# Layer normalisation on one core: tiles of 12 rows in place of 8, and a second first load on another queue

## The chip, the core and the metric

The kernel runs on one core of a Trainium2 chip. The metric is the device time of one execution, in microseconds (us). Before the change the median of three runs is 317.96 us (317.96 to 318.17).

## The reference

The input x has 32 x 512 rows of 1024 float32 values. Each row is normalised by its own mean and variance; there is no scale and no offset.

```python
mean = np.mean(x, axis=-1, keepdims=True)
var = np.var(x, axis=-1, keepdims=True)
return ((x - mean) / np.sqrt(var + eps)).astype(np.float32)      # eps = 1e-5
```

So 16384 rows of 4 KB, 67.11 MB, are read once and written once.

## The kernel before

**Tiles.** "Rows" of a tile are counted per partition. A tile of K rows is 128 x K rows of x, laid so that each of the 128 partitions holds K rows that lie one after the other in memory (`rows_of`, L58): for each partition one run of 4K KB, on both sides of a transfer. `TILES` (L10) lists the 20 tiles: 2, 2, 4, then fourteen of 8, then 4, 2, 2; together 128 rows per partition.

**Ring.** All tiles live in one buffer `ring` of 48 rows per partition (L55). `place` (L17) gives each tile its position, from the front again when the end is reached. A tile is normalised in place and stored from where it lies, so a load may start only when the stores of the tiles that lay in its rows have landed.

**Order.** The kernel is written under a manual schedule: each engine carries out its own instructions in the order of the program, and waits on semaphores for the others. For each tile the loop at L121 to L126 issues the load from SP's queue (L122), works on the tile in one group of up to 8 rows (`group`, L71), and issues the store from ScalarE's queue (L126). SP has nothing but loads, so it runs ahead as far as the ring lets it. In what follows L0, L1, ... are the loads and S0, S1, ... the stores of the tiles, counted from 0.

**A group of G rows.**
1. VectorE takes the statistics of each half row, 2G instructions (L75, `stats`).
2. GpSimd (POOL) joins the four partial means and sums of squares of each row in nine small instructions in a row (L64 to L100, `half`, `nmean`, `dev`, `ss`).
3. ScalarE takes the square root (L103, `std`), VectorE the reciprocal (L107, `rstd`), POOL the product of the mean and the reciprocal (L109, `nmr`).
4. ScalarE scales and shifts each row in place, G instructions (L111).

VectorE's reciprocal stands in its order ahead of the next tile's statistics, so VectorE waits in step 2 of each tile. The small tiles come from a pool with four buffers of each (`st`, L49).

Of the kernel before, what the change touches and what calls it, by code (L numbers as in the profile page):

```python
# [1 line left out]

# [4 lines left out]


TILES = (2, 2, 4) + (8,) * 14 + (4, 2, 2)  # L10

RING = 48

GROUP = 8


def place(tiles, ring):  # L17

    plan, row, pos = [], 0, 0
    for K in tiles:  # L20
        if pos + K > ring:
            pos = 0
        plan.append((K, row, pos))
        row += K
        pos += K
    return plan


@with_exitstack
def kernel(  # L30
    ctx: ExitStack,
    tc: tile.TileContext,
    x: bass.AP,
    eps: bass.AP,
    out: bass.AP,
):
    nc = tc.nc
    P = nc.NUM_PARTITIONS
    eps_val = float(eps) if not isinstance(eps, bass.AP) else 1e-5

    x2 = x.flatten_outer_dims()
    o2 = out.flatten_outer_dims()
    N, D = x2.shape
    BN_MAX = nc.vector.BN_STATS_FMAX
    NSUB = D // BN_MAX
    assert sum(TILES) * P == N

    rings = ctx.enter_context(tc.tile_pool(name="rings", bufs=1))
    st = ctx.enter_context(tc.tile_pool(name="st", bufs=4))  # L49

    fdt = mybir.dt.float32
    AF = mybir.ActivationFunctionType
    ALU = mybir.AluOpType

    ring = rings.tile([P, RING, D], fdt)  # L55
    eps_t = rings.tile([P, 1], fdt)

    def rows_of(a, row, K):  # L58
        return a[row * P : (row + K) * P].rearrange("(p k) d -> p k d", p=P)

    def pool_sum(o, terms):
        G = terms.shape[1]
        half = st.tile([P, GROUP, 2], fdt, name="half")
        nc.gpsimd.tensor_tensor(  # L64
            out=half[:, :G], in0=terms[:, :, 0:2], in1=terms[:, :, 2:4], op=ALU.add
        )
        nc.gpsimd.tensor_tensor(  # L67
            out=o, in0=half[:, :G, 0], in1=half[:, :G, 1], op=ALU.add
        )

    def group(xs, G):  # L71
        stats = st.tile([P, GROUP, NSUB, 6], fdt, name="stats")
        for k in range(G):
            for s in range(NSUB):
                nc.vector.bn_stats(  # L75
                    out=stats[:, k, s, :],
                    in_=xs[:, k, s * BN_MAX : (s + 1) * BN_MAX],
                )

        H = 2 * NSUB  # L80
        parts = stats[:, :G].rearrange("p g s (h c) -> p g (s h) c", h=2)
        mean4, m2 = parts[:, :, :, 1], parts[:, :, :, 2]
        nmean = st.tile([P, GROUP], fdt, name="nmean")
        dev = st.tile([P, GROUP, H], fdt, name="dev")
        ss = st.tile([P, GROUP], fdt, name="ss")
        pool_sum(nmean[:, :G], mean4)
        nc.gpsimd.tensor_scalar(  # L87
            out=nmean[:, :G], in0=nmean[:, :G], scalar1=-1.0 / H, scalar2=None, op0=ALU.mult
        )
        nc.gpsimd.tensor_tensor(  # L90
            out=dev[:, :G],
            in0=mean4,
            in1=nmean[:, :G].unsqueeze(2).to_broadcast([P, G, H]),
            op=ALU.add,
        )
        nc.gpsimd.tensor_mul(out=dev[:, :G], in0=dev[:, :G], in1=dev[:, :G])  # L96
        nc.gpsimd.tensor_scalar(  # L97
            out=dev[:, :G], in0=dev[:, :G], scalar1=float(D // H), scalar2=None, op0=ALU.mult
        )
        nc.gpsimd.tensor_tensor(out=dev[:, :G], in0=dev[:, :G], in1=m2, op=ALU.add)  # L100
        pool_sum(ss[:, :G], dev[:, :G])
        std = st.tile([P, GROUP], fdt, name="std")
        nc.scalar.activation(  # L103
            out=std[:, :G], in_=ss[:, :G], func=AF.Sqrt, bias=eps_t, scale=1.0 / D
        )
        rstd = st.tile([P, GROUP], fdt, name="rstd")
        nc.vector.reciprocal(out=rstd[:, :G], in_=std[:, :G])  # L107
        nmr = st.tile([P, GROUP], fdt, name="nmr")
        nc.gpsimd.tensor_mul(out=nmr[:, :G], in0=nmean[:, :G], in1=rstd[:, :G])  # L109
        for k in range(G):  # L110
            nc.scalar.activation(  # L111
                out=xs[:, k, :],
                in_=xs[:, k, :],
                func=AF.Identity,
                bias=nmr[:, k : k + 1],
                scale=rstd[:, k : k + 1],
            )

    with tc.manual_schedule():
        nc.vector.memset(eps_t, eps_val)  # L120
        for K, row, pos in place(TILES, RING):  # L121
            nc.sync.dma_start(out=ring[:, pos : pos + K, :], in_=rows_of(x2, row, K))  # L122
            for g in range(0, K, GROUP):
                G = min(GROUP, K - g)
                group(ring[:, pos + g : pos + g + G, :], G)
            nc.scalar.dma_start(out=rows_of(o2, row, K), in_=ring[:, pos : pos + K, :])  # L126


# [1 line left out]
_INS = ['x', 'eps']  # L130
_OUTS = [((32, 512, 1024), 'float32')]

_NUMBERS = {'eps': 1e-05}


# [26 lines left out]
```

## Time and profile before

| What | us | Where it is from |
|---|---|---|
| median of three runs | 317.96 | the times |
| the profiled execution | 317.86 | the times |
| its span, first to last instruction or packet | 316.1 | the page |
| VectorE busy | 157.1 | the page, engines |
| ScalarE busy | 154.3 | the page, engines |
| POOL busy | 45.1 | the page, engines |
| statistics of 8 rows, 16 instructions | 9.59 | the timeline of VectorE |
| scaling of 8 rows, 8 instructions | 9.16 | the timeline of ScalarE |
| an 8-row load, issue to landing, median | 47.3 | the page, DMA issues |
| an 8-row store, issue to landing, median | 40.7 | the page, DMA issues |

The span is shorter than the execution's own time by 1.76 us, which lies outside of what the profile follows. Queue q1 holds the loads that SP issues, q10 the stores that ScalarE issues; 16 DMA engines move the packets of both. Beside the page, the trace holds a record of each DMA packet with its queue, size, start and duration. A transfer of K rows per partition appears there as 128 packets of 4K KB, 8 on each engine, and a packet of 4 bytes on each engine that tells of completion.

### The profile page before, as it was taken

The page shows a single profiled execution, that of the slowest core. Times are in us where ns is not written, and L with a number is a line of the kernel's source. Part 1 is how long each engine was busy: PE and PEld are TensorE (multiplying, and loading weights), DVE is VectorE, ACT ScalarE, POOL GpSimd, SP SyncE. Part 2 cuts the span into 40 slices and gives each one's busy share as a digit, 9 for nine tenths or more (in the row PEclk, how much of TensorE's full clock was granted, in tenths as well). Part 3 has the DMA queues.
Part 4 walks back from the last instruction along what each step waited for, and adds up shares of the span by engine and source line. Part 5 has one row for each costly group of instructions (what it writes and reads, how often), then busy time and mean ns, then how long its engine had stood idle before and what let it go on. Part 6 is the DMA issues. An engine that isn't in the chain of part 4 may idle for free.

```text
span 316.1 us, 794 instructions
## 1 busy us (share of the span) xinstructions
DVE 157.1 (50%) x277; ACT 154.3 (49%) x149; POOL 45.1 (14%) x204
## 2 busy tenths in 40 slices
DVE  2368596547092561916529074190652908363030
ACT  1336296692833809247091561900651956196321
POOL 0420202201102020020200202002020020221120
DMA  7999999999999999999999999999999999999996
GB/s 301 433 399 469 431 416 425 433 427 444 420 448 419 444 419 444 435 427 444 419 448 415 448 424 440 423 448 419 444 423 440 423 435 429 446 428 417 455 411 282
DMA packets 5766, 134.27 MB, mean 425 GB/s; under 512 B 640, under 2 KB 640, under 8 KB 640
## 3 DMA queue, kind: packets, MB, share of 16 engines
q1 hardware_dynamic: 2880, 67.11, 49.6%
q10 hardware_dynamic: 2880, 67.11, 49.3%
q14 instruction: 6, 0.05, 0.0%
HBM read 67.11 MB, written 67.11 MB: 425 GB/s over the span
## 4 chain that ended last, share of the span: by engine, by line
DMA 58%; DVE 17%; ACT 9%; POOL 6%; issue 3%; another core or an unknown queue 3%; ACTq 0%; POOLq 0%; DVEq 0%; SPq 0%
DMA ring<-in_x_dram 32%; DMA out_dram<-ring 27%; DVE stats L75 17%; ACT ring L111 8%; POOL half L64 1%; ACT std L103 1%; POOL dev L97 1%; POOL nmean L87 1%; POOL dev L100 1%; POOL dev L90 1%; POOL dev L96 1%; POOL nmean L67 1%; POOL ss L67 1%; DVE rstd L107 0%
## 5 line engine op out<-in xcount | busy, mean ns | idle before, releaser
L75 DVE BATCH_NORM_STATS2 stats<-ring 128x6 f32<-128x512 f32 x256 | 153.7, 678 | 71.2 <-DMA ring<-in_x_dram 71.2
L111 ACT ACTIVATE ring<-ring,nmr,rstd 128x1024 f32<-128x1024 f32 x128 | 147.0, 1227 | 10.8 <-POOL nmr L109 10.8
L103 ACT ACTIVATE std<-ss,eps_t 128x8 f32<-128x8 f32 (+2 forms) x20 | 6.0, 300 | 143.0 <-POOL ss L67 115.8
L107 DVE RECIPROCAL rstd<-std 128x8 f32<-128x8 f32 (+2 forms) x20 | 3.9, 193 | 77.3 <-ACT std L103 77.3
L64 POOL TENSOR_TENSOR half<-stats 128x16 f32<-128x16 f32 (+2 forms) x20 | 4.5, 226 | 221.0 <-DVE stats L75 221.0
L109 POOL TENSOR_TENSOR nmr<-nmean,rstd 128x8 f32<-128x8 f32 (+2 forms) x20 | 4.0, 202 | 27.2 <-DVE rstd L107 27.2
L97 POOL TENSOR_SCALAR dev<-dev 128x32 f32<-128x32 f32 (+2 forms) x20 | 5.6, 281 | 1.8
L100 POOL TENSOR_TENSOR dev<-dev,stats 128x32 f32<-128x32 f32 (+2 forms) x20 | 4.9, 243 | 1.7
L90 POOL TENSOR_TENSOR dev<-stats,nmean 128x32 f32<-128x32 f32 (+2 forms) x20 | 4.6, 231 | 1.7
L87 POOL TENSOR_SCALAR nmean<-nmean 128x8 f32<-128x8 f32 (+2 forms) x20 | 4.6, 228 | 1.8
L96 POOL TENSOR_TENSOR dev<-dev 128x32 f32<-128x32 f32 (+2 forms) x20 | 4.6, 228 | 1.6
L64 POOL TENSOR_TENSOR half<-dev 128x16 f32<-128x16 f32 (+2 forms) x20 | 4.2, 210 | 1.6
L67 POOL TENSOR_TENSOR nmean<-half 128x8 f32<-128x8 f32 (+2 forms) x20 | 4.0, 199 | 1.6
L67 POOL TENSOR_TENSOR ss<-half 128x8 f32<-128x8 f32 (+2 forms) x20 | 4.0, 199 | 1.6
L103 ACT ACT_TABLE_LOAD x1 | 1.3, 1283 | 0.9 <-DVE eps_t L120 0.9
L120 DVE MEMSET eps_t<- 128x1 f32 x1 | 0.1, 59 | 0.8 <-PEq L143 0.8
L143 POOL MEMSET const-float32-0.0<- 128x1 f32 x1 | 0.1, 98 | 0.2 <-issue 0.2
L143 POOL MEMSET const-uint8-127<- 128x1 uint8 x1 | 0.1, 102 | 0.0
L143 POOL MEMSET const-bfloat16-1.0<- 128x1 bf16 x1 | 0.1, 101 | 0.0
L143 POOL MEMSET const-float32-1.0<- 128x1 f32 x1 | 0.1, 98 | 0.0
## 6 DMA issues: line engine op xcount, KB each, us to landing
ring<-in_x_dram SPq DMA_DIRECT2D x14, 4096.0 KB, 47.3
out_dram<-ring ACTq DMA_DIRECT2D x14, 4096.0 KB, 40.7
ring<-in_x_dram SPq DMA_DIRECT2D x4, 1024.0 KB, 30.8
ring<-in_x_dram SPq DMA_DIRECT2D x2, 2048.0 KB, 27.2
out_dram<-ring ACTq DMA_DIRECT2D x4, 1024.0 KB, 16.7
out_dram<-ring ACTq DMA_DIRECT2D x2, 2048.0 KB, 24.5
```

The source lines that it names most:

```text
L64: nc.gpsimd.tensor_tensor(out=half[:, :G], in0=terms[:, :, 0:2], in1=terms[:, :, 2:4], op=ALU.add)
L67: nc.gpsimd.tensor_tensor(out=o, in0=half[:, :G, 0], in1=half[:, :G, 1], op=ALU.add)
L75: nc.vector.bn_stats(out=stats[:, k, s, :], in_=xs[:, k, s * BN_MAX : (s + 1) * BN_MAX],)
L87: nc.gpsimd.tensor_scalar(out=nmean[:, :G], in0=nmean[:, :G], scalar1=-1.0 / H, scalar2=None, op0=ALU.mult)
L90: nc.gpsimd.tensor_tensor(out=dev[:, :G], in0=mean4, in1=nmean[:, :G].unsqueeze(2).to_broadcast([P, G, H]), op=ALU.add,)
L96: nc.gpsimd.tensor_mul(out=dev[:, :G], in0=dev[:, :G], in1=dev[:, :G])
L97: nc.gpsimd.tensor_scalar(out=dev[:, :G], in0=dev[:, :G], scalar1=float(D // H), scalar2=None, op0=ALU.mult)
L100: nc.gpsimd.tensor_tensor(out=dev[:, :G], in0=dev[:, :G], in1=m2, op=ALU.add)
L103: nc.scalar.activation(out=std[:, :G], in_=ss[:, :G], func=AF.Sqrt, bias=eps_t, scale=1.0 / D)
L107: nc.vector.reciprocal(out=rstd[:, :G], in_=std[:, :G])
L109: nc.gpsimd.tensor_mul(out=nmr[:, :G], in0=nmean[:, :G], in1=rstd[:, :G])
L111: nc.scalar.activation(out=xs[:, k, :], in_=xs[:, k, :], func=AF.Identity, bias=nmr[:, k : k + 1], scale=rstd[:, k : k + 1],)
```

## The change

- The tiles are 4, 8, then nine of 12, then 6 and 2: 13 tiles in place of 20. The ring keeps 48 rows, four tiles of 12.
- A group takes up to 12 rows (`GROUP`). In the last four tiles (`LAST`) a group takes up to 6 (`FINE`), so the last two tiles of 12 are worked on in two groups each, with one store for both. There are 15 groups in place of 20.
- The first two loads are issued ahead of the loop, that of the second tile (8 rows) from ScalarE's queue, beside the first (4 rows) from SP's queue. The other loads stay on SP's queue.
- All small tiles but `stats` move to a pool with 15 buffers of each (`sm`).
- `place` is written out in the function, and `H` is computed outside of `group`; both give the same as before.

```diff
-TILES = (2, 2, 4) + (8,) * 14 + (4, 2, 2)
+TILES = (4, 8, 12, 12, 12, 12, 12, 12, 12, 12, 12, 6, 2)
 
 RING = 48
 
-GROUP = 8
+GROUP = 12
+FINE = 6
+LAST = 4
...
     st = ctx.enter_context(tc.tile_pool(name="st", bufs=4))
+    sm = ctx.enter_context(tc.tile_pool(name="sm", bufs=len(TILES) + 2))
...
-        half = st.tile([P, GROUP, 2], fdt, name="half")
+        half = sm.tile([P, GROUP, 2], fdt, name="half")
...
-        nmean = st.tile([P, GROUP], fdt, name="nmean")
-        dev = st.tile([P, GROUP, H], fdt, name="dev")
-        ss = st.tile([P, GROUP], fdt, name="ss")
+        nmean = sm.tile([P, GROUP], fdt, name="nmean")
+        dev = sm.tile([P, GROUP, H], fdt, name="dev")
+        ss = sm.tile([P, GROUP], fdt, name="ss")
...
+    def load(queue, K, row, pos):
+        queue.dma_start(out=ring[:, pos : pos + K, :], in_=rows_of(x2, row, K))
...
     with tc.manual_schedule():
         nc.vector.memset(eps_t, eps_val)
-        for K, row, pos in place(TILES, RING):
-            nc.sync.dma_start(out=ring[:, pos : pos + K, :], in_=rows_of(x2, row, K))
-            for g in range(0, K, GROUP):
-                G = min(GROUP, K - g)
+        for t, (K, row, pos) in enumerate(plan[:2]):
+            load(nc.scalar if t == 1 else nc.sync, K, row, pos)
+        for t, (K, row, pos) in enumerate(plan):
+            if t > 1:
+                load(nc.sync, K, row, pos)
+            step = FINE if t >= len(TILES) - LAST else GROUP
+            for g in range(0, K, step):
+                G = min(step, K - g)
                 group(ring[:, pos + g : pos + g + G, :], G)
             nc.scalar.dma_start(out=rows_of(o2, row, K), in_=ring[:, pos : pos + K, :])
```

`std`, `rstd` and `nmr` move to `sm` in the same way.

More of the change, by code (lines that the diff above doesn't have):

```diff
@@ L7 @@
 from concourse._compat import with_exitstack
-TILES = (2, 2, 4) + (8,) * 14 + (4, 2, 2)
+TILES = (4, 8, 12, 12, 12, 12, 12, 12, 12, 12, 12, 6, 2)
 RING = 48
-GROUP = 8
[L17 to L26, printed above, removed]
+GROUP = 12
+FINE = 6
+LAST = 4
 @with_exitstack
@@ L45 @@
     NSUB = D // BN_MAX
+    H = 2 * NSUB
     assert sum(TILES) * P == N
@@ L78, in group @@
                 )
-        H = 2 * NSUB
         parts = stats[:, :G].rearrange("p g s (h c) -> p g (s h) c", h=2)
         mean4, m2 = parts[:, :, :, 1], parts[:, :, :, 2]
-        nmean = st.tile([P, GROUP], fdt, name="nmean")
-        dev = st.tile([P, GROUP, H], fdt, name="dev")
-        ss = st.tile([P, GROUP], fdt, name="ss")
+        nmean = sm.tile([P, GROUP], fdt, name="nmean")
+        dev = sm.tile([P, GROUP, H], fdt, name="dev")
+        ss = sm.tile([P, GROUP], fdt, name="ss")
         pool_sum(nmean[:, :G], mean4)
@@ L101, in group @@
         pool_sum(ss[:, :G], dev[:, :G])
-        std = st.tile([P, GROUP], fdt, name="std")
+        std = sm.tile([P, GROUP], fdt, name="std")
         nc.scalar.activation(
@@ L105, in group @@
         )
-        rstd = st.tile([P, GROUP], fdt, name="rstd")
+        rstd = sm.tile([P, GROUP], fdt, name="rstd")
         nc.vector.reciprocal(out=rstd[:, :G], in_=std[:, :G])
-        nmr = st.tile([P, GROUP], fdt, name="nmr")
+        nmr = sm.tile([P, GROUP], fdt, name="nmr")
         nc.gpsimd.tensor_mul(out=nmr[:, :G], in0=nmean[:, :G], in1=rstd[:, :G])
@@ L117, in group @@
             )
+    def load(queue, K, row, pos):
+        queue.dma_start(out=ring[:, pos : pos + K, :], in_=rows_of(x2, row, K))
+    plan, row, pos = [], 0, 0
+    for K in TILES:
+        if pos + K > RING:
+            pos = 0
+        plan.append((K, row, pos))
+        row += K
+        pos += K
     with tc.manual_schedule():
         nc.vector.memset(eps_t, eps_val)
-        for K, row, pos in place(TILES, RING):
-            nc.sync.dma_start(out=ring[:, pos : pos + K, :], in_=rows_of(x2, row, K))
-            for g in range(0, K, GROUP):
-                G = min(GROUP, K - g)
+        for t, (K, row, pos) in enumerate(plan[:2]):
[6 more added lines that the diff above has]
+                G = min(step, K - g)
                 group(ring[:, pos + g : pos + g + G, :], G)
```

## The prediction

> **What bounds the kernel now.** I read the page first, its spans, engine shares and the two DMA rows:
>
> ```profile
> span 316.1 us, 794 instructions
> ...
> DVE 157.1 (50%) x277; ACT 154.3 (49%) x149; POOL 45.1 (14%) x204
> ...
> DMA  7999999999999999999999999999999999999996
> GB/s 301 433 399 469 431 416 425 433 427 444 420 448 419 444 419 444 435 427 444 419 448 415 448 424 440 423 448 419 444 423 440 423 435 429 446 428 417 455 411 282
> ...
> q1 hardware_dynamic: 2880, 67.11, 49.6%
> q10 hardware_dynamic: 2880, 67.11, 49.3%
> ```
>
> No compute engine is busy for more than half of the span, and every DMA slice but the first and the last shows a 9. The two queues (q1 loads, q10 stores) fill 98.9% of the 16 engines' time. Next I asked for busy times by stretch (span start, us in it, busy time of DVE, ACT, POOL, clock, DMA share, GB/s):
>
> ```profile
> 18.00:58.00 40.00, 30.53 (x54) 23.30 (x24) 6.78 (x30) 1.00 1.00 426
> 58.00:300.00 242.00, 117.43 (x206) 123.11 (x118) 32.03 (x140) 1.00 1.00 433
> ```
>
> The DMA share is 1.00 in both. Then the waits of the engines and of SP's queue:
>
> ```profile
> DVE stats L75 <- DMA ring<-in_x_dram: 71.2, 13, 7.3
> ...
> SPq L122 <- DMA out_dram<-ring: 215.6, 12, 19.0
> ```
>
> VectorE waits for loads, and loads wait for stores to free the ring; no line has a DMA engine waiting for compute. The kernel is bounded by the sum of its packets on each DMA engine. From the records of single packets the first one starts between 1.76 and 2.84 us (mean of the 16 engines 2.35), the last ends at 314.9, and the span ends 1.2 us after that.
>
> **What the Trainium skill says.** (1) "DMA: Bandwidth & Descriptors", section "Queues, rings and completion order": each engine takes turns between its queues, one packet at a time. The trace agrees: between 90 and 220 us, load and store packets of equal size hold 50.4% and 49.7%. (2) Same page, "Issuing engines are not separate DMA queues": a second issuing engine adds no DMA capacity. In this trace the loads alone already fill the engines (2 to 18 us: share 1.01, 425 GB/s). (3) Same page, "At most 65,535 descriptors per engine (HWDGE)": one descriptor moves one contiguous run, and only a row over 64 KiB is spoken of as being cut. A run here grows from 32 to 48 KB; no trace yet shows 48 KB.
>
> **The price of a packet.** A transfer of K rows per partition is 128 packets of 4K KB, 8 per engine, and one 9-ns completion packet on each engine. From the first completion packets of successive transfers I get time per packet: two-row stores at 308.31, 310.77, 313.22 give 2.455/8 = 0.306 us per 8 KB; the four-row store from 303.45 to 308.31 gives 0.607 per 16 KB; nine load-and-store pairs from 84.72 to 259.28 us give 19.396 each, less 0.018, over 16 = 1.211 per 32 KB. The line through these is 0.302 us per 8 KB plus 0.004 per packet. (The recorded durations, 309, 611 and 1213 ns, overlap by 2 to 4 ns; with them the fixed part would be 8 ns.) The page's section "Why small descriptors are slow" prices a packet's fixed part at about 3 cycles; with its 850 MHz fabric clock that is an estimate of 3.5 ns, in agreement with 4. So 48 KB should take 6 x 0.3018 + 0.004 = 1.815 us and 24 KB 0.909.
>
> **The change part by part.**
>
> *Tile sizes.* Before, per engine and both queues: 14 tiles of 8 rows, 224 x 1.211 = 271.3; two of 4, 32 x 0.607 = 19.4; four of 2, 64 x 0.306 = 19.6; 40 completions 0.4: **310.6 us**. After: nine of 12, 144 x 1.815 = 261.3; one of 8, 19.4; one of 4, 9.7; one of 6, 16 x 0.909 = 14.5; one of 2, 4.9; 26 completions 0.2: **310.1 us**. That is 112 packets and 14 completions fewer, **-0.55 us**, all on the path. With the recorded durations it is -1.1, the lower bound. Check on before: 2.35 + 310.6 + 1.1 (early packets that took longer than their kind, 17.6 us over 16 engines) = 314.1; engines end from 313.2 to 314.9.
>
> *The head: L0 (4 rows, SP) beside L1 (8 rows, ACT).* The two alternate, 8 x (0.607 + 1.211) = 14.5 us, so both land near 16.9, where before had its first tile at 5.3. The engines carry loads meanwhile, so this costs nothing while work is queued. Is it? SP issues L0, L2, L3, L4 without a wait; L5 overlaps tiles 0 and 1, so it waits for stores S0 and S1. The work queued without S2 and L5 is 8 x (0.607 + 1.211 + 3 x 1.815) = 58.1 of loads, 4.9 of S0, 9.7 of S1: it lasts until 2.35 + 72.7 = **75.0 us**. S2 is reached by these rows:
>
> ```profile
> 37.51 9.59 DVE L75 BATCH_NORM_STATS2 stats<-ring 128x6 f32<-128x512 f32 x16
> ...
> 37.91 9.16 ACT L111 ACTIVATE ring<-ring,nmr,rstd 128x1024 f32<-128x1024 f32 x8 [0.55 <-POOL nmr L109]
> 47.10 0.34 ACTq L126 DMA_DIRECT2D out_dram<-ring  x1
> ```
>
> That is 0.6 us per half row on VectorE and 1.146 per row on ScalarE. From the end of one tile's statistics to the start of the next is 3.3 (34.18 to 37.51), to the first scaled row 3.7, 0.2 more for 12 rows. Start 17.3 (landing + 0.4, as 5.31 to 5.69). Tile 0: 4.8, 3.2, to 25.3. Tile 1: 9.6, 3.3, to 38.2. Tile 2: 14.4 to 52.6; scaling from 56.5, 12 x 1.146, to **70.3**; S2 moves from 71.3 (first load: issue 0.72, packet 1.76). Cover 3.7 us. L5 follows S1's landing at about 77.5; S2's own 14.5 us cover that. S0 leaves at 30 and S1 at 48, before anything needs them.
>
> *ScalarE's queue.* The L1 issue (0.34 us) goes ahead of the table load and delays it; ScalarE's first real work was at 10.78 before and is near 25 now. Nothing is behind it that is needed earlier. SP and POOL are moved past nothing.
>
> *Steady state.* A load waits for the store four tiles back. The loop is load 29 us, statistics 14.4, chain 3.9, scaling 13.8, store 29, two issues of about 1.5: 93 us against 4 x 29.05 = 116. VectorE needs 17.8 of every 29 us. If that cover were gone, each us over 116 would be shown once per four tiles.
>
> *The tail.* The last four tiles go in groups of 6 and 2. S12's compute takes what S19's took, 8.8 us (landing 300.29, issue 309.08); L12 lands no later than S9, which it rides beside, and then S10 and S11, 8 x (1.815 + 0.909) = 21.8 us, are still to go. Cover 13 us; before had 1.7 (309.08 against 310.77).
>
> *Groups and buffers.* 15 chains in place of 20, and 15 small buffers in place of 4: no listed wait is for such a buffer, and POOL is busy 14%. Nothing. ScalarE's two long waits for a load (26.8 us, stores leaving at 223.28 and 242.63) lie in slices with the DMA full: their loss gains nothing.
>
> **Sum.** -0.55 us. The profiled execution took 317.86 (span 316.1 + 1.76), 0.1 under the median of 317.96. Forecast **317.4**, span 315.5.
>
> **Not shown by the trace.** The 48-KB packet: lower bound the line (1.815, or -1.1 us in all with the recorded durations); upper, a cut into 32 + 16 KB, 1.818, 144 x 0.003 + 0.1 completions = +0.5, so about 0 in all; I take the line. Loads side by side on two queues, and 12-row loads early: 62 of the 67 slow 32-KB packets start before 58 us, up to 0.5 us longer each, cause not shown; with the 8-KB ones they cost 1.1 us per engine. None at all would give up to -1.1 more; as much again, +1.1. I take no change. The spread of the engines' ends (1.7 us) can move by as much as half a us either way.
>
> **Rivals.**
> 1. *The early slow packets shrink* because the first 30 us hold other shapes: -0.55 - 0.85 = 316.5. For it: they cluster at 15.8 to 22.3 and 42 to 57 us, stages that change. Against: no cause is visible. 10%.
> 2. *The packet is cut, or the gain is lost in the ends' spread*: 317.9. For: no 48-KB packet seen. Against: 8, 16 and 32 KB each came as one. 8%.
> 3. *Slower: a 48-KB packet runs below the line.* Place: 144 packets on every engine. Price: 1 ns more on each is 0.14 us. From (0.55 + 0.64)/144 = 8.3 ns, 0.5% over 1.815, it decides for slower; at 1% (18 ns) it gives 320.0. For: run length and row pitch are new. Against: 24 KB more per packet changed nothing from 8 to 32 KB. 9%.
> 4. *The DMA runs dry near 75 us* because S2 is late. Cover 3.7 us, then 1 us for each; slower from 4.9 us late; at 6, 319.7. For: the first tile starts 11.6 us later than before. Against: every duration has a row. 5%.
>
> **How the numbers follow.** A measurement here can tell about 0.2% (0.64 us), so the bounds are 317.32 and 318.60. The main case (68%) has its centre just inside "same" and spreads by about 0.8: 0.32 faster, 0.31 same, 0.05 slower. Rival 1 adds 0.10 to faster; rival 2 adds 0.06 to same and 0.02 to slower; rivals 3 and 4 are 0.14 slower. In all 0.42, 0.37, 0.21. Cases of both signs hold the chance; the main case's own range is 316.6 to 318.2. Out to rivals 1 and 2 and the near part of 3: 316.2 to 318.8.
>
> **What would show it.** Right: 1872 packets per queue, DMA row of 9s without a hole near 75 us, S2 issued near 70, L0 landing near 17, a load-and-store pair every 29.05 us, the last store issued several us ahead of the one before it landing. Wrong: packets above 1872 (cut), a pair above 29.2 us (rival 3), a DMA slice under 9 in mid-span (rival 4), or a span under 314.5 (rival 1).

## The result, and the profile after

The changed kernel takes **319.29 us** (median of four runs, 319.11 to 319.55) against 318.06 for the kernel before beside it: ratio 1.0039, interval 1.0022 to 1.0056. It is slower by 1.2 us; the forecast was 317.4 with a range to 318.8. The profiled execution took 319.27 us.

The page of the changed kernel, the same rows as were shown of before:

```profile
span 317.3 us, 685 instructions
...
DVE 155.9 (49%) x272; ACT 152.2 (48%) x144; POOL 35.4 (11%) x154
...
DMA  7999999999999999999999999999999999999995
GB/s 318 454 417 471 388 397 443 450 421 448 384 434 430 428 452 409 440 446 434 415 434 440 440 415 434 446 441 421 434 434 446 409 415 446 439 445 426 434 412 234
...
q10 hardware_dynamic: 2016, 71.30, 52.1%
q1 hardware_dynamic: 1728, 62.92, 46.4%
```

Still a 9 in every slice between the first and the last: the DMA never ran dry (in the packet records every whole microsecond from 4 to 313 us is at least 97% full). The packets are 3744 (q10 now holds one load, so they aren't 1872 each), 2016 fewer than before; each run of 48 KB came as one packet. And yet the two queues fill 98.5% of a span that is longer by 1.2 us. The engines moved the same bytes, in fewer packets, in more time.

The waits of the changed kernel (first for which, us in all, times, longest):

```profile
DVE stats L68 <- DMA ring<-in_x_dram: 96.1, 10, 18.9
...
SPq L112 <- DMA out_dram<-ring: 228.8, 8, 36.6
```

As before, compute waits for loads and loads for stores, in longer pieces. The head went as it was worked out; ScalarE's timeline has S2's issue, forecast for 70.3:

```profile
57.08 13.69 ACT L103 ACTIVATE ring<-ring,nmr,rstd 128x1024 f32<-128x1024 f32 x12 [0.59 <-POOL nmr L101]
70.80 0.34 ACTq L133 DMA_DIRECT2D out_dram<-ring  x1
```

Where the time went is seen in the busy times by stretch (the last two columns are DMA share and GB/s), first for the stretches that were shown of before:

```profile
18.00:58.00 40.00, 30.35 (x54) 15.62 (x16) 6.96 (x30) 1.00 0.99 420
58.00:300.00 242.00, 125.30 (x217) 132.68 (x125) 27.42 (x116) 1.00 1.01 433
```

GB/s divided by share is the rate "at full share", while all 16 engines are busy. The share is printed to 0.01, which is about 2 GB/s and too coarse for these long stretches; the packet records give 424.5 before 58 us and 430.5 after it (before the change 424.6 and 431.3). The loss shows in the later stretch alone, and plainly only in a short piece of it. Before the change:

```profile
80.00:92.00 12.00, 5.31 (x10) 9.46 (x9) 0.20 (x1) 1.00 1.00 432
```

and changed:

```profile
80.00:92.00 12.00, 10.18 (x18) 8.59 (x8) 1.33 (x6) 1.00 0.99 397
```

432 against 401 at full share: there the packets take longer than their kind. I call the excess over the usual duration of a size the *long packets*, summed over the records and divided by 16 engines. They are 1.13 us per engine before and 2.46 after, and they come in **episodes** of 4 to 20 us. The trace does not number the engines; what the table says of single engines comes from stringing packets together, and is good to about 0.1 us.

| us per engine, from packet records | before | before again | changed | changed again | one queue | one queue again |
|---|---|---|---|---|---|---|
| packet sum at the usual durations | 310.6 | 310.6 | 310.1 | 310.1 | 310.1 | 310.1 |
| mean first packet start, plus long packets before 8 us | 2.54 | 2.58 | 2.54 | 2.58 | 2.75 | 2.85 |
| long packets, 8 to 50 us | 0.60 | 0.64 | 0.72 | 0.72 | 0.87 | 0.55 |
| long packets, 50 to 110 us | 0.19 | 0.12 | **0.91** | **1.03** | 0.07 | 0.08 |
| long packets after that | 0.12 | 0.11 | 0.36 | 0.20 | 0.50 | 0.22 |
| last engine's end less the mean end | 1.1 | 1.2 | 1.8 | 1.2 | 1.6 | 2.6 |
| span | 316.1 | 316.2 | 317.3 | 316.7 | 316.7 | 317.3 |

Changed less before, first profiles: packets -0.56, long packets after 8 us +1.08, uneven ends +0.7, after the last packet +0.09: +1.3 for a measured +1.2 (records overlap by a few ns, which leaves 0.1 to 0.2 unplaced). In the second profiles: -0.56, +1.08, 0.0 and +0.13, together +0.65 for a measured +0.5. The start costs nothing: where the first packets begin earlier they take longer.

### The profile page after: what moved, and what is told of

The parts are those of the page before. It is cut to its first block, busy times and chain, and to the rows that moved or that the text cites. A ratio compares the mean times of both kernels' runs of the same rounds, so it can differ in the third digit from the quotient of the medians.

```text
span 317.3 us, 685 instructions
## 1 busy us (share of the span) xinstructions
DVE 155.9 (49%) x272; ACT 152.2 (48%) x144; POOL 35.4 (11%) x154
## 3 DMA queue, kind: packets, MB, share of 16 engines
q10 hardware_dynamic: 2016, 71.30, 52.1%
## 4 chain that ended last, share of the span: by engine, by line
DMA 66%; DVE 15%; ACT 8%; POOL 4%; issue 2%; SPq 0%; POOLq 0%; DVEq 0%
DMA ring<-in_x_dram 43%; DMA out_dram<-ring 23%; DVE stats L68 14%; ACT ring L103 8%; POOL half L57 1%; POOL dev L89 1%; ACT std L95 0%; POOL dev L92 0%; POOL nmean L79 0%; POOL dev L82 0%; POOL dev L88 0%; POOL nmean L60 0%; POOL ss L60 0%; DVE rstd L99 0%; POOL nmr L101 0%
## 5 line engine op out<-in xcount | busy, mean ns | idle before, releaser
L95 ACT ACTIVATE std<-ss,eps_t 128x12 f32<-128x12 f32 (+4 forms) x15 | 4.5, 301 | 142.3 <-POOL ss L60 142.3
L57 POOL TENSOR_TENSOR half<-stats 128x24 f32<-128x24 f32 (+4 forms) x15 | 3.6, 237 | 246.4 <-DVE stats L68 246.4
L99 DVE RECIPROCAL rstd<-std 128x12 f32<-128x12 f32 (+4 forms) x15 | 3.1, 207 | 48.7 <-ACT std L95 48.7
L89 POOL TENSOR_SCALAR dev<-dev 128x48 f32<-128x48 f32 (+4 forms) x15 | 4.4, 294 | 1.3
L101 POOL TENSOR_TENSOR nmr<-nmean,rstd 128x12 f32<-128x12 f32 (+4 forms) x15 | 3.1, 206 | 9.8 <-DVE rstd L99 9.8
L92 POOL TENSOR_TENSOR dev<-dev,stats 128x48 f32<-128x48 f32 (+4 forms) x15 | 3.9, 262 | 1.3
L82 POOL TENSOR_TENSOR dev<-stats,nmean 128x48 f32<-128x48 f32 (+4 forms) x15 | 3.7, 248 | 1.2
L88 POOL TENSOR_TENSOR dev<-dev 128x48 f32<-128x48 f32 (+4 forms) x15 | 3.6, 242 | 1.2
L79 POOL TENSOR_SCALAR nmean<-nmean 128x12 f32<-128x12 f32 (+4 forms) x15 | 3.6, 239 | 1.3
L57 POOL TENSOR_TENSOR half<-dev 128x24 f32<-128x24 f32 (+4 forms) x15 | 3.2, 215 | 1.2
```

The lines of the kernel that those rows point to most:

```text
L57: nc.gpsimd.tensor_tensor(out=half[:, :G], in0=terms[:, :, 0:2], in1=terms[:, :, 2:4], op=ALU.add)
L79: nc.gpsimd.tensor_scalar(out=nmean[:, :G], in0=nmean[:, :G], scalar1=-1.0 / H, scalar2=None, op0=ALU.mult)
L82: nc.gpsimd.tensor_tensor(out=dev[:, :G], in0=mean4, in1=nmean[:, :G].unsqueeze(2).to_broadcast([P, G, H]), op=ALU.add,)
L89: nc.gpsimd.tensor_scalar(out=dev[:, :G], in0=dev[:, :G], scalar1=float(D // H), scalar2=None, op0=ALU.mult)
L95: nc.scalar.activation(out=std[:, :G], in_=ss[:, :G], func=AF.Sqrt, bias=eps_t, scale=1.0 / D)
```

## The experiments

The ratio is to the kernel before in the same session.

**1 and 14, one queue**, the same kernel twice:

```diff
-            load(nc.scalar if t == 1 else nc.sync, K, row, pos)
+            load(nc.sync, K, row, pos)
```

> The changed kernel with L1 back on SP's queue, behind L0; all else as changed. The theories of the extra 1.2 us, all of which agree that it is in DMA packets that take longer than their kind (2.46 us per engine after, 1.13 before) and in the engines' uneven ends. Theory A, the restart: the load queue is empty from 75 to 81 us because L5 waits for S0 and S1, and when loads start again beside stores, packets run long (0.9 us per engine at 80 to 92) and the engines spread by 2.4 us. Here L0 lands near 7, S0 and S1 leave about 10 us earlier, L5 arrives before L4 ends, and the restart is gone: 317.3 to 317.9. Theory B, long packets: 48-KB load packets are what runs long in the first 100 us, wherever the loads come from: 318.8 to 319.3. Theory C, the two queues at the start set the engines in lockstep: 317.3 to 317.9.

> The changed kernel with all loads on SP's queue, once more. If its lack of an episode between 50 and 110 us (0.07 us per engine) follows from the program: 0.3 or less again, and 317.9 to 318.8. If it was chance: 0.7 or more, 318.8 to 319.5.

Measured: 318.45 (ratio 1.0021, 1.0008 to 1.0034), and 320.02 (1.0049, 1.0037 to 1.0062). The times scatter, over both, from 317.75 to 320.33; 3 of 13 were over 319 the first time and 14 of 18 the second. The first median lies between the forecasts, the second above both of its own. The two profiles, though, agree with each other. Same stretch, first and second profile:

```profile
80.00:92.00 12.00, 8.64 (x15) 10.46 (x10) 0.00 (x0) 1.00 0.94 406
```

```profile
80.00:92.00 12.00, 9.08 (x16) 9.92 (x9) 0.00 (x0) 1.00 0.93 401
```

The GB/s are as low as in the changed kernel, but so is the share (a packet counts wholly in the stretch in which it starts): 432 and 431 at full share. So the episode at 80 to 92 us hangs on ScalarE's queue for L1, as A and C said. The two are not told apart, since the edit also keeps the load queue from running empty (L5 is issued at 70.6 us, before L4 ends at 82.9). Compute beside the DMA does not explain the episode: VectorE and ScalarE together were as busy in this stretch (19.1 us) as in the changed kernel (18.8). The time does not follow the episode. In the second profile only 0.85 us of long packets are left after 8 us, no more than before the change, and the last engine ends 2.6 us after the mean. Undoing the second queue does not bring the time back reliably; neither profile is of an execution near 320 us (they took 318.45 and 319.10), so what makes those slow is not shown.

**2, the ring refilled by 4 and 8 rows**, and **3, 12-row tiles between the old ends**:

```diff
-TILES = (4, 8, 12, 12, 12, 12, 12, 12, 12, 12, 12, 6, 2)
+TILES = (4, 8, 12, 12, 12, 4, 8, 12, 12, 12, 12, 12, 6, 2)          # 2, L1 on ScalarE's queue
+TILES = (2, 2, 4, 4) + (12,) * 9 + (4, 2, 2)                        # 3, one queue, LAST = 5
```

> The changed kernel, still with L1 on ScalarE's queue, but the ring is refilled by a load of 4 and a load of 8 rows (tiles 4, 8, 12, 12, 12, 4, 8, five of 12, 6, 2), so the first refill waits for S0 alone and is queued near 55 us, before L4 ends. Theory A (restart): the empty load queue near 75 us is gone, and with it the long packets of 80 to 92: 317.6 to 318.3, with 16 packets per engine more at 0.004 us. Theory B (48-KB packets): still nine tiles less one of 12 rows early, 319.0 to 319.4. Theory C (two queues at the start): 319.0 to 319.4.

> The 12-row tiles between small first and last tiles as before the change (2, 2, 4, 4, nine of 12, 4, 2, 2), all loads on SP. Packet sum 310.2 us per engine against 310.6 before. Theory A: the refill waits for four small stores that leave early, no restart: 317.3 to 317.9. Theory B: 318.6 to 319.3. Theory C: 317.3 to 317.9.

Measured: 321.72 (1.0126, 1.0099 to 1.0152), and 322.57 (1.0152, 1.0137 to 1.0168); outside of what any theory said. In the second experiment the load queue no longer runs empty near 75 us, and long packets between 50 and 110 us are 1.31 us per engine, 0.9 of it at 96 to 100 us: A is not enough. The third lost most of its time at the end, a thing of its own; between 50 and 110 us it has 0.65 us of long packets. ScalarE's timeline of it:

```profile
300.09 0.34 ACTq L133 DMA_DIRECT2D out_dram<-ring  x1
...
313.42 0.34 ACTq L133 DMA_DIRECT2D out_dram<-ring  x1
```

and its last stretches:

```profile
305.00:310.00 5.00, 2.47 (x4) 0.00 (x0) 1.68 (x9) 1.00 0.97 413
310.00:315.00 5.00, 0.17 (x1) 2.67 (x3) 0.38 (x2) 1.00 0.39 165
```

The last 2-row load took turns with 48-KB stores, landed at 304.65, and its store left at 313.42, when the other stores were through on 14 of the 16 engines: the DMA share falls to 0.39, which is 3 us of idle engines.

**4, tiles of 8 rows with the changed first tiles**, and **6, the same on one queue**:

```diff
+TILES = (4, 8) + (8,) * 13 + (4, 4, 2, 2)      # GROUP = FINE = 8; 6: all loads on SP
```

> No 48-KB packets: tiles of 8 rows in the ring of 48, but the first two tiles as changed (4 rows on SP, 8 rows on ScalarE's queue beside it), thirteen more of 8, then 4, 4, 2, 2. The first refill of 8 rows waits for S0 and S1, and the load queue runs empty near 70 us as in the changed kernel. Theory A: the restart with 32-KB packets costs about two thirds of that with 48 KB: 318.5 to 319.0. Theory B: no 48-KB packets, as before, 317.8 to 318.2. Theory C: 318.7 to 319.3.

> Tiles of 8 rows with first tiles of 4 and 8, as the fourth experiment, but all loads on SP's queue. Theory C (queue): as before the change, 317.8 to 318.3. Theory D (sizes of the first tiles): 319.0 to 319.8 as the fourth experiment, with 0.6 us per engine or more at the start and as much where the stores join.

Measured: 319.62 (1.0050, 1.0037 to 1.0063), above all three ranges, and 323.67 (1.0177, 1.0157 to 1.0196; median of four executions, and two more took 329.76 and 336.31). Experiment 4 in the same stretch:

```profile
80.00:92.00 12.00, 7.49 (x14) 8.54 (x9) 2.32 (x10) 1.00 1.01 412
```

408 at full share, and 1.18 us of long packets between 50 and 110 us, with no packet over 32 KB: the episode needs no 12-row tile, and B falls as the sole cause. Experiment 6 fits no range: long packets all along (0.84 us between 50 and 110 us, not in one episode, and 1.8 after 110), late loads on the last engine up to 12 us behind those on the first, and so a last load that landed at 308.98. The last two stores:

```profile
309.22 0.34 ACTq L133 DMA_DIRECT2D out_dram<-ring  x1
...
317.75 0.34 ACTq L133 DMA_DIRECT2D out_dram<-ring  x1
```

Its time is in part that late last store; the profile is of an execution of 324.35 us, so 336 is not explained. But the long packets between 50 and 110 us are there on one queue: with tiles of 8 rows the larger first tiles bring them without the second queue.

**5, the old tiles with two queues** (the second 2-row load beside the first):

```diff
+            queue = nc.scalar if t == 1 else nc.sync
+            queue.dma_start(out=ring[:, pos : pos + K, :], in_=rows_of(x2, row, K))
```

> The kernel before, with one edit: its second load (2 rows) goes out on ScalarE's queue beside the first. The extra time so far lies in three episodes of long load packets: at the start, where the first stores join, and where stores and loads of equal size meet (76 to 92 us). Theory C, the two queues cause the third episode (it stood in all three kernels with two queues and in none with one): 318.7 to 319.5, with over 0.5 us per engine of long packets between 50 and 100 us. Theory D, the sizes of the first tiles (4 and 8 in place of 2, 2, 4) make the episodes long, the queue does not: 317.9 to 318.3, the profile as before.

Measured: 318.25 (1.0006, 0.9999 to 1.0014); 0.06 us of long packets between 50 and 110 us. The second queue by itself is harmless. It mattered with the larger first tiles and 12-row tiles (1 and 14), and was not needed with the larger first tiles and 8-row tiles (6).

**7, the old first tiles before 12-row tiles, changed last tiles**:

```diff
+TILES = (2, 2, 4, 4) + (12,) * 9 + (6, 2)      # one queue
```

> The 12-row tiles and the changed kernel's last tiles (6, 2), but first tiles 2, 2, 4, 4 on SP's queue: the third experiment without its late last store (there the last 2-row load rode beside 48-KB store packets and its store left at 313.4, with the engines idle before it). Theories C and D: only the head cost time, so this keeps the saved packets: 317.3 to 317.9. Theory E, tiles of 12 rows by themselves spread the engines' ends (5 us at load 13 of the third experiment against 2.2 before), and the last engine sets the end: 318.6 to 320, with ends over 2.5 us apart.

Measured: 319.05 (1.0034, 1.0022 to 1.0046). Long packets between 50 and 110 us 0.75, last end 2.5 us after the mean; its stretch, 418 at full share:

```profile
80.00:92.00 12.00, 7.91 (x14) 6.42 (x8) 2.52 (x10) 1.00 0.96 401
```

As E said, 12-row tiles cost time without the changed first tiles and on one queue. The load queue runs empty here too (L6 ends at 72.8, L7 is issued at 77.6).

**8 and 15, the changed kernel and the kernel before once more**, no edit:

> The changed kernel once more, to see what of its profile comes back. If the episodes of long packets follow from the program: total long-packet time 2.2 to 2.7 us per engine, again an episode at 80 to 92 us of 0.7 to 1.1, and 319.1 to 319.6. If they are chance: the total differs by more than 0.5 us and the times scatter by more than 1 us.

> The kernel before, once more, for its profile: long packets after 8 us 0.7 to 1.1 us per engine (0.91 in the first), 0.3 or less between 50 and 110 us, 317.8 to 318.3, if its low figure belongs to the program.

Measured: 319.17 (1.0047, 1.0034 to 1.0059) and 318.08 (1.0002, 0.9993 to 1.0011). The changed kernel's second profile:

```profile
80.00:92.00 12.00, 10.38 (x18) 8.65 (x8) 1.22 (x5) 1.00 0.98 406
92.00:110.00 18.00, 0.23 (x1) 13.99 (x13) 1.30 (x6) 1.00 1.02 432
```

The long packets between 50 and 110 us come back in size (0.91 and 1.03, table above), and so does the low figure of the kernel before: the sum belongs to the program. Their place does so in part: of 0.88 us at 80 to 92 in the first profile 0.56 came back there, less than was expected, and 0.44 stood at 96 to 106, where the first had 0.03. The uneven ends do not come back (1.8 and 1.2), and the changed kernel's times scatter (318.57 to 320.34), as was expected of chance.

**9, the kernel before with a ring of 32**:

```diff
-RING = 48
+RING = 32
```

> The kernel before with one edit: a ring of 32 rows in place of 48. Same packets, one queue, same first tiles; but L6 must wait for the first three stores (near 52 us) while the loads in hand end near 49, so the load queue is empty for some 5 us and loads start again beside stores, as in the changed kernel at 75 to 81. Theory A, the restart makes the episode of long packets after 50 us: 0.5 us per engine or more between 50 and 110 us (0.19 before), 318.5 to 319.2. Rival S, the episode needs engines that run in step from a start with larger tiles, and the gap does nothing: 0.3 or less, 317.9 to 318.3.

Measured: 317.92 (0.9994, 0.9988 to 1.0001). L6 was issued at 52.4, after L5's end at 49.8, so the load queue did run empty (to 56.3), and 0.08 us of long packets followed. A falls for 32-KB packets: a restart needs something else beside it. The kernel before needs only two thirds of its ring.

**10, a stagger**:

```diff
+        nc.sync.dma_start(
+            out=ring[0:8, 36:42, :], in_=x2[0:48].rearrange("(p k) d -> p k d", p=8)
+        )
```

> The changed kernel with one more small load behind L0: 8 partitions of 24 KB, one packet of 0.91 us on 8 of the 16 engines, into rows of the ring that L4 writes later; those engines run 0.9 us behind the others from then on. The output is not touched. Theory S (engines in step make the long packets, being out of step ends them): long packets after 8 us fall from 1.9 to 2.0 us per engine (two profiles) to 1.2 or less; the time is 318.6 to 319.4, since eight engines carry 0.9 us more. Theory A (restart): no change, 1.7 to 2.2, and 319.6 to 320.4.

Measured: 322.27 (1.0146, 1.0118 to 1.0173), above both ranges. The edit did far more than to set engines apart. Its stretches at the extra load and at the old episode:

```profile
16.00:22.00 6.00, 1.59 (x3) 0.00 (x0) 0.00 (x0) 1.00 1.00 229
...
80.00:92.00 12.00, 12.00 (x21) 11.09 (x10) 0.00 (x0) 1.00 1.01 401
```

229 GB/s at full share: eight packets that read 192 KB of neighbouring rows, and wrote them to eight neighbouring partitions, took up to 3.3 us in place of 0.91, and the 48-KB load packets beside them up to 4.5 in place of 1.8. Which of the two sides does it was not tried. The engines were well out of step afterwards (they end L3 2.1 us apart, 0.9 without the extra load), and the episode at 80 to 92 us was there in full (1.02 us between 50 and 110). S falls.

**11, the old head, then 12-row tiles**, the one I hoped would beat both:

```diff
+TILES = (2, 2, 4) + (8,) * 5 + (12,) * 6 + (6, 2)      # one queue
```

> A version that may beat both: the first 48 rows as before the change (2, 2, 4, five of 8, one queue), then six tiles of 12, then 6 and 2. Packet sum 310.3 us per engine (before 310.6, changed 310.1). Its loads run out once, late: L10 waits for a store that lands near 139 while L9 ends near 134. Theory A: an episode of long packets at 140 to 155 us of 0.3 us or more, 318.2 to 318.9. Theory S (the engines have long been out of step by then): no episode, 317.4 to 318.0.

Measured: 318.55 (1.0014, 1.0006 to 1.0022), from 317.91 to 320.09. Its profiled execution took 317.94, with 0.95 us of long packets after 8 us and 0.03 between 130 and 160: in this execution 48-KB packets in the steady part were harmless, also where the load queue ran empty (134.8 to 143.7 us). So the profile is as S said, while the median lies in A's range; the execution profiled is one of the shortest, and what the others add is not shown. Over 21 runs it is not faster than the kernel before, but slower by 0.1%.

**12 and 13, tiles stored in reverse order**, changed and before:

```diff
-            nc.scalar.dma_start(out=rows_of(o2, row, K), ...
+            nc.scalar.dma_start(out=rows_of(o2, N // P - row - K, K), ...
```

> The changed kernel with one edit: tile t is stored at the mirrored place of the output (last rows first), so the output's tiles are in reverse order; packets, queues, waits and compute are the same, and only the addresses of stores against loads differ. Theory T (long packets come from loads and stores that meet in unlucky places of memory): the episode at 80 to 92 us goes or moves, long packets after 8 us change by more than 0.5 us per engine, and the time moves with it, below 318.7 or above 320. Rival P (the pattern of queues and sizes makes them, wherever the data lie): 1.7 to 2.3 again, 0.7 or more of it between 50 and 110 us, 318.9 to 319.6.

> The kernel before with the same edit (tiles stored in reverse order). Theory T: what was a lucky placing is gone; long packets after 8 us move from 0.9 by 0.4 us or more per engine, 318.6 to 319.6. Rival P: 0.7 to 1.1, 317.8 to 318.3.

Measured: 319.89 (1.0053, 1.0041 to 1.0065) and 318.11 (1.0000, 0.9992 to 1.0008). The episode stands where it first stood; the changed kernel's stretch reads

```profile
80.00:92.00 12.00, 10.26 (x18) 8.63 (x8) 1.25 (x5) 1.00 1.01 414
```

410 at full share; 2.27 and 0.96 us of long packets after 8 us. The profiles are as P said in both (the changed kernel's time lies between the two ranges): which tile of the output meets which load does not matter at this scale. The addresses that the loads read were left as they were.

## Why the prediction was wrong, point by point

- *What bounds the kernel* was right: the DMA row and the waits agree that the sum of packet time on the last engine sets the end, and so do the profiles of the experiments but 3 and 6, where a late last store adds to it.
- *The price of a packet* was right. From L6 to L9 a load-and-store pair took 29.03 us (first completion packets at 137.86 and 224.94), forecast 29.05; a 48-KB packet is 1.813 us, forecast 1.815. So the -0.55 us were saved (with the recorded durations the line gives -1.0 and not the -1.1 of the lower bound; nothing rests on it). Rival 3 did not happen. Of rival 2, no packet was cut, but the ends' spread did eat the gain in the first profile (+0.7), and not in the second.
- *The head* was right in time: L0 landed at 17.6 (forecast 16.9), S2 was issued at 70.80 (70.3), L5 at 77.0 (77.5). No hole near 75 us: rival 4 did not happen. *Tail*: last store at 304.17, S11's first landing at 310.8, cover 6.6 us and not 13, since the last load was later on the slowest engine (295.4). Still covered.
- *The step that failed* stands under "Not shown by the trace": long packets, "I take no change". They grew by 1.33 us in all and by 1.08 after the first 8 us, beyond what the -0.55 gained. The term had the right bound (+1.1 for as much again) and the wrong value, and the ends' spread, held at half a us either way, added 0.7 in the profiled execution and nothing in the second profile. Both bad ends together are 319.0 on the prediction's own arithmetic; the range stopped at 318.8, and the chance of slower rested on rivals 3 and 4, with only 0.05 from the main case and 0.02 from rival 2.
- The reason for that error: I took long packets as a trait of the early stage, with no cause, and did not ask what in the change touches that stage. The change rewrites it wholly: other first tiles, another queue, other sizes when stores join.

What the runs show of the cause: the extra long packets belong to the program (experiment 8) and mostly to the first 110 us. Two parts of the change can bring them on: larger first tiles with 8-row tiles (4 on two queues, 6 on one), and 12-row tiles early behind small first tiles (7, and 3). But the parts do not add: both together on one queue leave 0.07 and 0.08 us between 50 and 110 us (1 and 14), and only with the second queue 0.91 and 1.03. No single part is the cause. Not needed or not enough are the second queue (5), an empty load queue (2, 9, 11), being in step (10), and the order of output tiles (12). **Open** is what in the memory or the engines makes a packet long, and whether it hangs on where in memory the engines read at one time, which no run varied by itself; the records add only that loads carry over four times the excess that stores do (after 20 us 1.65 and 0.34 us per engine in the changed kernel, 0.55 and 0.05 before). Open too is what decides which engine ends last: with one queue the same program took 317.75 to 320.33 us.

## What to carry to other kernels

Where the DMA is full from end to end, fewer and larger transfers gain only their fixed part, 4 ns a packet here, and here that was lost to packets that ran long, most of them in the first hundred microseconds; divide GB/s by DMA share, stretch by stretch, to see it. Look at the last engine's end, not only at the mean. Let a small last load ride beside small stores: beside 48-KB stores it lands many us later, and the DMA waits for its store (experiment 3).

## What was not expected of the hardware

- Eight engines that moved 192 KB of neighbouring rows to eight neighbouring partitions at once took two to four times as long (up to 3.3 us for a packet of 0.91), and the other engines' loads beside them ran long too (experiment 10).
- Where one of the trace's few 8-KB packets of the kind "instruction" passes, a load packet beside it is longer by 0.2 to 0.6 us (5 of 6 in the kernel before, 4 of 4 in the changed kernel). When packets are strung together engine by engine, the engine with both of the packets longer by over 0.5 us ends last in the kernel before (314.9 us, mean near 313.8) and in the second one-queue profile (316.1, mean 313.4), but at the mean in the changed kernel (314.2). So they are not the whole of what decides the last end.
- The same program can scatter by 2.6 us (one queue) while another, with the same bytes, stays within 0.9 us over 39 runs (the kernel before).
